# Gate and up projections of three feed-forward groups by seven block products in place of eight

## The chip, the cores and the metric

The kernel runs on one NeuronCore of a Trainium2 chip. The time is device microseconds of one launch on that core; a kernel's time is the median of several runs. Engines are named as in the profile: PE (TensorE matmul), PEld (its weight load), DVE (VectorE), ACT (ScalarE), POOL (GpSimd), SP (SyncE, which issues most loads).

## The reference

A trunk of two layers on 256 tokens of width 1024, in float32:

```python
for l in range(DEPTH):
    x = x + 0.5 * swiglu(rms_norm(x, ffn1_norm[l]), ffn1_w_gate[l], ffn1_w_up[l], ffn1_w_down[l])
    ...   # projection, windowed and differential attention, output projection
    x = x + 0.5 * swiglu(rms_norm(x, ffn2_norm[l]), ffn2_w_gate[l], ffn2_w_up[l], ffn2_w_down[l])
return rms_norm(x, final_norm)

def swiglu(h, w_gate, w_up, w_down):
    return (jax.nn.silu(h @ w_gate) * (h @ w_up)) @ w_down
```

The feed-forward width is 2816. There are four feed-forwards in all, and the change touches only them.

## The kernel before

Every float32 matrix is used as a sum of two float32r parts, a high part (the rounded value) and a low part (what is left). A product of two such matrices takes three matmuls: high by high, low by high, high by low. One matmul has a 128x128 stationary block of activations (128 tokens) and 512 columns of weights as the moving operand; it adds into one PSUM bank of 128x512.

The 2816 columns of a feed-forward are cut into five groups of 512 and a rest of 256. For group n the main loop (line 642) computes gate and up of the 256 tokens (two banks each, `tokens`, line 470: 8 blocks of the inner dimension, 2 token halves, 3 matmuls, so 48 matmuls for gate and 48 for up), turns the hidden values of the group before (`turn`, line 609: eight PE transposes, then a split into high and low part by ACT and DVE), applies silu on ACT (`gate`) and the product with up on DVE (`up`, line 555), and adds the down product of the group before into four accumulator banks (`down`, line 623: two halves of 24 matmuls). PSUM has eight banks; four of them are the accumulators for the whole feed-forward.

Weights come as a list of steps, `specs`. A plain step is 1 MB: 512 rows by 512 columns. `emit_dma` (line 154) has SP load it into one of six `raw` buffers; `emit_split` (line 167) makes the high part on ACT (two casts of 128x1024, into one of three `whi` buffers) and the low part on DVE (two subtractions of 128x1024, into one of three `wlo` buffers). `weights()` (line 219) hands out the next step's parts, and before that calls `ahead`, which emits the splits up to two steps ahead (`LOOK`), the preparations (`prep`) one step further, and the loads up to eight steps ahead (`AHEAD`) as long as a `raw` buffer is to be had. PE, ACT, DVE and POOL instructions run on each engine in the order in which the program emits them, except in a part of the attention; so where `weights()` is called decides where the casts stand in ACT's and DVE's queues.

The kernel before already holds the code for seven products, but the tuple `SEVEN` (line 31) is empty, so `seven` (line 115), `by_seven` (line 575), `prod` (line 565) and `make_sums` (line 304) are never called. With `SEVEN` empty a group has six weight steps: gate upper and lower rows, up upper and lower rows, and the two halves of down.

Of the kernel before, what the change touches and what calls it, by code (L numbers as in the profile page):

```python
# [27 lines left out]
LOOK, AHEAD = 2, 8  # L28
N_RAW, N_HI, N_LO = 6, 3, 3
N_S4 = 16  # L30
SEVEN = ()


@with_exitstack
def trunk(ctx: ExitStack, tc: tile.TileContext, x, n1, g1, u1, d1, nm, w_in, sink,
# [31 lines left out]
    def nm_(s):  # L67
        uid[0] += 1
        return f"{s}_{uid[0]}"

    def bank():
        return ps.tile([P, 512], F32, tag="ps", bufs=8, name=nm_("ps"))

    def halves(b):
        return b.rearrange("p (a n) -> p a n", a=2)

    def blk(dt=F32R):
        return s4.tile([P, 2, 512], dt, tag="s4", name=nm_("s4"))

    def tmp(tag="tmp", bufs=5, shape=(P, 2, 256), dt=F32):  # L80
        return tp.tile(list(shape), dt, tag=tag, bufs=bufs, name=nm_(tag))
# [137 lines left out]
    def weights(look=LOOK):  # L219
        i = at["use"]  # L220
        at["use"] += 1
        if i > 1:
            ahead(i + look)
        return loaded.pop(i)

    for l in range(DEPTH):
        def ffn_specs(wg, wu, wd):
# [3 lines left out]
            for g in range(1, NGRP):  # L231
                downs = [down(g - 1, h) for h in range(2)]
                if g in SEVEN:
                    specs.extend(seven(wg[l], wu[l], g * 512, downs))
# [38 lines left out]
    class Norm:  # L273
# [30 lines left out]
        def make_sums(self):  # L304

            self.sm = []

            def part(b, t):

                vs = [f(self.xs[2 * b + i]) for i in range(2)]  # L310
                return [[v[:, :, c + t * P:c + (t + 1) * P] for v in vs] for c in (0, S)]

            def make(x, y, op, rest):
                v = tmp().rearrange("p a (c s) -> p (a c) s", c=2)
                for i in range(2):
                    vi = v[:, 2 * i:2 * i + 2]
                    dve.tensor_tensor(vi, x[i], y[i], op=op)
                    for z, o in rest:
                        dve.tensor_tensor(vi, vi, z[i], op=o)
                sm = blk().rearrange("p a (c s) -> p (a c) s", c=2)  # L320
                act.copy(sm[:, :, 0:P], v)
                dve.tensor_tensor(sm[:, :, P:S], v, f(sm[:, :, 0:P]), op=ALU.subtract)
                self.sm.append(sm)
                return [v[:, 0:2], v[:, 2:4]]

            add, sub = ALU.add, ALU.subtract
            (t0h, t0l), (t1h, t1l), (b0h, b0l), (b1h, b1l) = [part(b, t) for b in range(2) for t in range(2)]
            s1 = make(b1h, t1h, sub, [(b1l, add), (t1l, sub)])
            s2 = make(s1, t0h, add, [(t0l, add)])
            make(t1h, t0h, sub, [(t1l, add), (t0l, sub)])  # L330
            make(b0h, s2, sub, [(b0l, add)])

        def quarter(self, t, b):

# [48 lines left out]
    norm = Norm(0)  # L383
# [86 lines left out]
    def tokens(accs, xs, w, k0, ks=range(4), first=0, last=KC - 1, order=None):  # L470

        hi, lo = w
        for k, t in (order or [(k, t) for k in ks for t in range(2)]):
            kk = k0 + k
            xv = xs[kk // 2][:, kk % 2]
            xh, xl = xv[:, t * P:(t + 1) * P], xv[:, S + t * P:S + (t + 1) * P]
            pe.matmul(accs[t], lhsT=xh, rhs=hi[:, k], start=kk == first, stop=False)
            pe.matmul(accs[t], lhsT=xl, rhs=hi[:, k], start=False, stop=False)
            pe.matmul(accs[t], lhsT=xh, rhs=lo[:, k], start=False, stop=kk == (last if isinstance(last, int) else last[t]))
# [63 lines left out]
    def ffn(norm, aside=None, before=None, final=False):  # L543
        def silu(out_, acc, t):
            act.activation(out_, acc, AF.Silu, scale=norm.r[:, t:t + 1])
            return out_

        def gate(gs):
            g = []
            for t in range(2):  # L550
                n = gs[t].shape[1]
                g.append(silu(tmp().rearrange("p a n -> p (a n)")[:, :n], gs[t], t))
            return g

        def up(h, acc, g, t):
            n = acc.shape[1]
            dve.scalar_tensor_tensor(h[:, t, :n], in0=acc, scalar=norm.hr[:, t:t + 1], in1=g, op0=ALU.mult, op1=ALU.mult)

        def hidden(g, us):
            h = blk(F32)  # L560
            for t in range(2):
                up(h, us[t], g[t], t)
            return h

        def prod(xo):
            hi, lo = weights()
            acc = bank()
            for k in range(4):
                xh, xl = xo(k)
                pe.matmul(acc, lhsT=xh, rhs=hi[:, k], start=k == 0, stop=False)  # L570
                pe.matmul(acc, lhsT=xl, rhs=hi[:, k], start=False, stop=False)
                pe.matmul(acc, lhsT=xh, rhs=lo[:, k], start=False, stop=k == 3)
            return acc

        def by_seven(h, g):

            flat = lambda: tmp().rearrange("p a n -> p (a n)")

            def put(o, x, y, op):
                dve.tensor_tensor(o, x, y, op=op)  # L580
                return o

            p1 = prod(norm.quarter(0, 0))
            m1 = flat()
            act.copy(m1, p1)
            p7 = prod(norm.summed(2))
            hT = turn(h, 2)
            p6 = prod(norm.summed(1))
            u2 = put(flat(), p6, m1, ALU.subtract)
            u3 = put(flat(), p7, u2, ALU.add)  # L590
            down(hT, g - 1, 0, weights())
            h = blk(F32)
            p2 = prod(norm.quarter(0, 1))
            g0 = put(m1, p2, m1, ALU.add)
            silu(g0, g0, 0)
            p4 = prod(norm.quarter(1, 1))
            g1 = put(flat(), p4, u3, ALU.subtract)
            silu(g1, g1, 1)
            p5 = prod(norm.summed(0))
            put(u3, u3, p5, ALU.subtract)  # L600
            put(u2, u2, p5, ALU.subtract)
            up(h, u3, g1, 1)
            p3 = prod(norm.summed(3))
            put(u2, u2, p3, ALU.add)
            up(h, u2, g0, 0)
            down(hT, g - 1, 1, weights())
            return h

        def turn(hs, n):
            out_ = []  # L610
            for i in range(n):
                sl = halves(bank())
                for c in range(2):
                    for t in range(2):
                        pe.transpose(sl[:, c, t * P:(t + 1) * P], hs[:, t, (2 * i + c) * P:(2 * i + c + 1) * P], ident)
                hb = blk()
                split(hb, sl)
                out_.append(hb)
            return out_

        accs = [[bank(), bank()] for _ in range(2)]

        def down(hT, g, h, w):
            tokens(accs[h], [None] * (2 * g) + hT, w, 4 * g, last=(FC - 1, G4 - 1) if final and h else FC - 1)


        gs, us = [bank(), bank()], [bank(), bank()]
        if before is None:
            before = norm.late
        before(0)  # L630
        ws = (weights(), weights(LOOK - 1))
        for k in (0, 2):
            if k:
                before(1)
            for sl, w in zip((gs, us), ws):
                tokens(sl, norm.xs, w, 0, (k, k + 1))
        before(2)
        tokens(gs, norm.xs, weights(), 4)
        g = gate(gs)
        tokens(us, norm.xs, weights(), 4)  # L640
        h = hidden(g, us)
        for n in range(1, NGRP):
            if n + 1 == min(SEVEN, default=0):
                norm.make_sums()
            if n == 3 and aside is not None:
                aside()
            if n in SEVEN:
                h = by_seven(h, n)
                continue
            gs = [bank(), bank()]  # L650
            tokens(gs, norm.xs, weights(), 0)
            hT = turn(h, 2)
            tokens(gs, norm.xs, weights(), 4)
            g = gate(gs)
            us = [bank(), bank()]
            for k0 in (0, 4):
                tokens(us, norm.xs, weights(), k0)
            h = hidden(g, us)
            for hh in range(2):
                down(hT, n - 1, hh, weights())  # L660

        gu = [bank(), bank()]
        tokens(gu, norm.xs, weights(), 0)
        hT = turn(h, 2)
        tokens(gu, norm.xs, weights(), 4)
        h = hidden(gate([b[:, 0:256] for b in gu]), [b[:, 256:512] for b in gu])
        return accs, hT, lambda: turn(h, 1)
# [278 lines left out]
    for l in range(DEPTH):  # L946
# [7 lines left out]
        if not final:  # L954
            norm = Norm((l + 1) * 8)
# [71 lines left out]
```

## Time and profile before

| | us |
|---|---|
| median of 3 runs | 964.41 (964.31 to 964.84) |
| profiled execution | 964.2 |
| its span on the core | 962.4 |
| PE busy in the span | 951.3 |
| DVE busy | 557.4 |
| ACT busy | 478.2 |
| POOL busy | 20.1 |

Times in the views are microseconds from the start of the span. In a timeline row stand the start, the time of the merged instructions, the engine, the line (here always that of a helper, L50), the operation, output and input tiles, shapes, the count, and the idle time before with what ended it. In a row of grouped instructions stand the count, then busy time and mean nanoseconds of one, then idle time before. In a row of DMA issues stand the count, the size of one and the median time from issue to landing. In a row by stretches stand, for each engine, the busy time and the number of instructions, then the granted clock of PE, the share of time that the DMA engines were busy, and GB/s.

### The profile page before, as it was taken

The numbers are of one execution on the slowest core, as the hardware profiler recorded it, in microseconds if no ns is written. First come the engines' busy times: TensorE is split into PE (matmuls) and PEld (weight loads), VectorE is DVE, ScalarE is ACT, GpSimd is POOL, SyncE is SP. The second block draws the span as 40 slices with busy tenths as digits, with TensorE's granted clock in tenths as the row PEclk, the third lists the DMA queues.
The fourth block names the chain that finished last, engine by engine and source line by source line (L and its number), as shares of the span: only waits on it lengthen the run. The fifth ranks groups of instructions, "written<-read, shape, count | busy, mean of one in ns | idle before, by whom it ended". The sixth has DMA issues, their size and how long they took to land.

```text
span 962.4 us, 12393 instructions
## 1 busy us (share of the span) xinstructions
PE 951.3 (99%) x4940; PEld 807.9 (84%) x4940; DVE 557.4 (58%) x854; ACT 478.2 (50%) x781; POOL 20.1 (2%) x49
## 2 busy tenths in 40 slices
PE   8999999999999999999999999999999999999997
PEld 6888888899888888888888888888999888888886
DVE  5555545579756555545665445556796665445453
ACT  7544444467735543443554434435676464434443
POOL 0300000000000000000000000000000000000001
PEclk9999999999999999999999999999999999999998
DMA  9965555655425565555556555556551446565501
GB/s 338 329 218 175 177 187 204 176 176 132 132 91 173 188 205 179 192 188 185 174 180 210 179 185 198 183 176 179 172 174 47 161 150 214 175 227 189 175 1 44
DMA packets 98218, 169.39 MB, mean 176 GB/s; under 512 B 3182, under 2 KB 30896, under 8 KB 98160
## 3 DMA queue, kind: packets, MB, share of 16 engines
q1 hardware_dynamic: 96816, 167.27, 52.2%
q0 software_dynamic: 256, 0.29, 0.4%
q10 hardware_dynamic: 1088, 1.05, 0.3%
q8 instruction: 38, 0.62, 0.3%
q14 instruction: 20, 0.16, 0.0%
HBM read 167.54 MB, written 1.05 MB: 175 GB/s over the span
## 4 chain that ended last, share of the span: by engine, by line
PE 98%; DMA 0%; issue 0%; DVE 0%; ACT 0%; POOLq 0%; POOL 0%; ACTq 0%; DVEq 0%
PE ps L50 98%; DMA xk<-in_x_dram 0%; DVE s L50 0%; ACT tmp L50 0%; DVE xk L50 0%; POOLq L1022 0%; POOL rf L50 0%; ACTq L50 0%; DVE rf L50 0%; DVEq L50 0%
## 5 line engine op out<-in xcount | busy, mean ns | idle before, releaser
L50 PE MATMUL ps<-whi,s 128*128 128x512 f32 (+1 forms) x2316 | 717.5, 391 | 0.0
L50 DVE TENSOR_TENSOR wlo<-raw,whi 128x1024 fp32r<-128x1024 f32 (+2 forms) x392 | 378.6, 1014 | 237.7 <-ACT whi L50 234.7
L50 PEld LDWEIGHTS ps<-whi,s 128*128 128x128 f32 x2316 | 431.2, 188 | 87.2 <-ACT whi L50 0.3
L50 ACT CAST whi<-raw 128x1024 fp32r<-128x1024 f32 (+2 forms) x392 | 323.9, 884 | 264.0 <-PE ps L50 245.0
L50 PE MATMUL ps<-wlo,s 128*128 128x512 f32 x1158 | 450.2, 389 | 0.0
L50 PEld LDWEIGHTS ps<-wlo,s 128*128 128x128 f32 x1158 | 217.7, 188 | 45.4 <-DVE wlo L50 0.4
L50 PE MATMUL ps<-s,whi 128*128 128x256 f32 x448 | 82.7, 286 | 0.0
L50 ACT CAST s<-ps 128x512 fp32r<-128x512 f32 x48 | 26.0, 589 | 97.4 <-PE ps L50 97.4
L50 DVE TENSOR_TENSOR s<-ps,s 128x512 fp32r<-128x512 f32 x48 | 31.1, 687 | 72.9 <-ACT s L50 72.9
L50 PEld LDWEIGHTS ps<-s,whi 128*128 128x128 f32 x448 | 70.1, 192 | 1.1
L50 PE MATMUL ps<-s,wlo 128*128 128x256 f32 x224 | 63.3, 283 | 0.0
L50 ACT ACTIVATE tmp<-ps,r 128x512 f32<-128x512 f32 (+1 forms) x48 | 30.8, 654 | 46.9 <-PE ps L50 46.8
L50 DVE SCALAR_TENSOR_TENSOR s<-ps,hr,tmp 128x512 f32<-128x512 f32 (+1 forms) x48 | 32.4, 705 | 31.8 <-PE ps L50 25.4
L50 PEld LDWEIGHTS ps<-s,wlo 128*128 128x128 f32 x224 | 42.9, 192 | 0.0
L50 PE MATMUL ps<-ident,s 128*128 128x128 f32 x304 | 39.6, 273 | 0.0
L50 PEld LDWEIGHTS ps<-ident,s 128*128 128x128 f32 x304 | 35.1, 141 | 4.7
L50 ACT ACTIVATE s<-s,negm 128x256 f32<-128x256 f32 x64 | 31.9, 501 | 7.4 <-DVE negm L50 7.4
L50 ACT ACTIVATE s<-ps,gcol 128x256 fp32r<-128x256 f32 x48 | 19.3, 473 | 19.1 <-PE ps L50 19.0
L50 DVE SCALAR_TENSOR_TENSOR s<-ps,gcol,s 128x256 fp32r<-128x256 f32 x48 | 20.3, 477 | 12.5 <-ACT s L50 12.4
L50 POOL TENSOR_TENSOR r<-ms,mhalf 128x2 f32<-128x2 f32 x6 | 4.2, 707 | 629.9 <-DVE ms L50 629.9
L50 ACT ACTIVATE junk<-xk 128x512 f32<-128x512 f32 x24 | 15.3, 637 | 0.4
L50 PE MATMUL ps<-vA,s 128*128 128x64 f32 x128 | 14.7, 273 | 0.0
(93 smaller groups left out, 269.8 us busy)
## 6 DMA issues: line engine op xcount, KB each, us to landing
raw<-in_ffn_w_down_dram SPq DMA_DIRECT2D x44, 1024.0 KB, 4.9
raw<-in_ffn_w_gate_dram SPq DMA_DIRECT2D x39, 1024.0 KB, 5.0
raw<-in_ffn_w_up_dram SPq DMA_DIRECT2D x39, 1024.0 KB, 5.0
raw<-in_w_in_dram SPq DMA_DIRECT2D x14, 1024.0 KB, 5.1
raw<-in_ffn_w_gate_dram SPq DMA_DIRECT2D x8, 512.0 KB, 3.6
raw<-in_ffn_w_up_dram SPq DMA_DIRECT2D x8, 512.0 KB, 4.6
raw<-in_w_in_dram SPq DMA_DIRECT2D x8, 512.0 KB, 4.5
raw<-in_w_out_dram SPq DMA_DIRECT2D x4, 1024.0 KB, 4.8
```

Of the source, the lines that this page charges most:

```text
L50: ins = issue(*a, **k)
```

## The change

In groups 2, 3 and 4 of every feed-forward, gate and up are computed together as a product of a 2x2 block matrix of activations (token half by half of the inner dimension) with a 2x2 block matrix of weights, by Winograd's form of Strassen's method: seven block products of 12 matmuls each (`prod`), where the plain way takes eight.

With a the gate's upper rows, b and c the up's upper and lower rows, and d the gate's lower rows, the nine weight steps of such a group are, in order: a (product p1), b+c (p7), a+b+c (p6), the first half of down, d (p2), a+b+c+d (p4), a+b (p5), c (p3), the second half of down. b+c is made by a load of b and an accumulating DMA of c onto it, issued by POOL (`gather`, line 125; it is emitted right behind b's load). a+b+c and a+b+c+d are made by DVE (`plus`, line 130: two additions of 128x1024 each). a+b is made by another accumulating DMA from POOL, of b onto a, emitted after a's cast and after the addition that reads a. So b and c are read from HBM twice.

On the activations' side, four sums of token and inner-dimension blocks are made once for each feed-forward (`make_sums`): on DVE 20 operations of 256 columns, four low parts of 512, on ACT four casts of 512. The change emits them in four portions between the steps of group 1.

The products are combined by one ACT copy and seven DVE operations of 128x512 (`put`), and silu and `up` follow as before.

Against the code that is there, three things are changed: `SEVEN` is set to (2, 3, 4); `make_sums` becomes a generator whose portions are emitted one by one in group 1; and in `by_seven` the call of `weights()` is taken out of `prod`, so that from p2 on the next step's casts are emitted ahead of silu and `up`, while the copy of p1's bank and the sums u2 and u3 stay ahead of the casts that follow them.

```diff
-SEVEN = ()
+SEVEN = (2, 3, 4)
...
             s1 = make(b1h, t1h, sub, [(b1l, add), (t1l, sub)])
+            yield
             s2 = make(s1, t0h, add, [(t0l, add)])
+            yield
             make(t1h, t0h, sub, [(t1l, add), (t0l, sub)])
+            yield
             make(b0h, s2, sub, [(b0l, add)])
+            yield
...
-        def prod(xo):
-            hi, lo = weights()
+        def prod(xo, w):
+            hi, lo = w
             acc = bank()
...
-            p1 = prod(norm.quarter(0, 0))
+            p1 = prod(norm.quarter(0, 0), weights())
             m1 = flat()
             act.copy(m1, p1)
-            p7 = prod(norm.summed(2))
+            p7 = prod(norm.summed(2), weights())
             hT = turn(h, 2)
-            p6 = prod(norm.summed(1))
+            p6 = prod(norm.summed(1), weights())
             u2 = put(flat(), p6, m1, ALU.subtract)
             u3 = put(flat(), p7, u2, ALU.add)
             down(hT, g - 1, 0, weights())
             h = blk(F32)
-            p2 = prod(norm.quarter(0, 1))
+            p2 = prod(norm.quarter(0, 1), weights())
             g0 = put(m1, p2, m1, ALU.add)
+            w = weights()
             silu(g0, g0, 0)
-            p4 = prod(norm.quarter(1, 1))
+            p4 = prod(norm.quarter(1, 1), w)
             g1 = put(flat(), p4, u3, ALU.subtract)
+            w = weights()
             silu(g1, g1, 1)
-            p5 = prod(norm.summed(0))
+            p5 = prod(norm.summed(0), w)
             put(u3, u3, p5, ALU.subtract)
             put(u2, u2, p5, ALU.subtract)
+            w = weights()
             up(h, u3, g1, 1)
-            p3 = prod(norm.summed(3))
+            p3 = prod(norm.summed(3), w)
             put(u2, u2, p3, ALU.add)
+            w = weights()
             up(h, u2, g0, 0)
-            down(hT, g - 1, 1, weights())
+            down(hT, g - 1, 1, w)
             return h
...
         for n in range(1, NGRP):
-            if n + 1 == min(SEVEN, default=0):
-                norm.make_sums()
+            sums = norm.make_sums() if n + 1 == min(SEVEN, default=0) else iter(())
...
             g = gate(gs)
+            next(sums, None)
             us = [bank(), bank()]
             for k0 in (0, 4):
                 tokens(us, norm.xs, weights(), k0)
+                next(sums, None)
             h = hidden(g, us)
             for hh in range(2):
                 down(hT, n - 1, hh, weights())
+                if hh == 0:
+                    next(sums, None)
```

## The prediction

> **What bounds the kernel now.** I read the page's busy shares and chain first, then the busy time by stretches for groups 2 to 4 of the first feed-forward, then the timelines of PE, DVE and ACT in the same place, then the groups by shape, the DMA queues and the waits of SP's queue.
>
> ```profile
> span 962.4 us, 12393 instructions
> PE 951.3 (99%) x4940; PEld 807.9 (84%) x4940; DVE 557.4 (58%) x854; ACT 478.2 (50%) x781; POOL 20.1 (2%) x49
> PE 98%; DMA 0%; issue 0%; DVE 0%; ACT 0%; POOLq 0%; POOL 0%; ACTq 0%; DVEq 0%
> ```
>
> ```profile
> core 0: us, PE busy (x) PEld busy (x) DVE busy (x) ACT busy (x) POOL busy (x), PEclk, DMA share, GB/s
> 103.30:136.80 33.50, 33.50 (x153) 27.86 (x152) 17.78 (x17) 15.53 (x17) 0.00 (x0) 1.00 0.59 192
> 136.80:170.30 33.50, 33.50 (x153) 27.84 (x152) 16.88 (x16) 14.25 (x16) 0.00 (x0) 1.00 0.56 190
> ```
>
> ```profile
> 103.33 1.03 PE L50 MATMUL ps<-ident,s 128*128 128x128 f32 x8
> 104.12 0.71 PE L50 MATMUL ps<-whi,s 128*128 128x512 f32 x2
> 104.67 0.39 PE L50 MATMUL ps<-wlo,s 128*128 128x512 f32 x1
> 104.90 0.62 PE L50 MATMUL ps<-whi,s 128*128 128x512 f32 x2
> 105.35 0.39 PE L50 MATMUL ps<-wlo,s 128*128 128x512 f32 x1
> 105.58 0.62 PE L50 MATMUL ps<-whi,s 128*128 128x512 f32 x2
> ```
>
> The whole chain is PE, so each matmul that goes is worth its pitch as long as PE is fed. Three matmuls start every 105.58 - 104.90 = 0.68 us, 0.227 each. A group of 144 matmuls takes 32.64 us, and its eight transposes some 0.86 (103.33 to 104.12, and a longer first matmul behind them): 33.5, the stretch that repeats at the full clock. DVE works 16.88 us of that, so it idles half the time. The reader is to see that half: it is what the change spends.
>
> ```profile
> 104.58 1.29 DVE L50 TENSOR_TENSOR s<-ps,s 128x512 fp32r<-128x512 f32 x2 [0.38 <-ACT s L50]
> 106.02 2.36 DVE L50 TENSOR_TENSOR wlo<-raw,whi 128x1024 fp32r<-128x1024 f32 x2
> 111.52 2.36 DVE L50 TENSOR_TENSOR wlo<-raw,whi 128x1024 fp32r<-128x1024 f32 x2 [3.14 <-ACT whi L50]
> 120.06 1.43 DVE L50 SCALAR_TENSOR_TENSOR s<-ps,hr,tmp 128x512 f32<-128x512 f32 x2 [1.54 <-PE ps L50]
> L50 DVE TENSOR_TENSOR wlo<-raw,whi 128x1024 fp32r<-128x1024 f32 x256 | 302.1, 1222 | 227.6 <-ACT whi L50 224.6
> L50 DVE TENSOR_TENSOR s<-ps,s 128x512 fp32r<-128x512 f32 x48 | 31.1, 687 | 72.9 <-ACT s L50 72.9
> L50 DVE TENSOR_TENSOR wlo<-raw,whi 128x256 fp32r<-128x256 f32 x32 | 11.1, 419 | 0.0
> 103.96 1.07 ACT L50 CAST s<-ps 128x512 fp32r<-128x512 f32 x2 [1.21 <-PE ps L50]
> 109.18 1.37 ACT L50 ACTIVATE tmp<-ps,r 128x512 f32<-128x512 f32 x2 [0.94 <-PE ps L50]
> 110.44 1.99 ACT L50 CAST whi<-raw 128x1024 fp32r<-128x1024 f32 x2
> ```
>
> **PE's part of the change.** Gate and up of a group take 84 matmuls in place of 96; the down products and transposes stay. A group goes from 33.5 to 132 x 0.227 + 0.86 = 30.8 us. Three groups in four feed-forwards: 12 x 2.72 = 32.6 us is the most there is to gain.
>
> **ACT's part.** Nine weight steps in place of six, at 1.99 us a pair of casts, give 17.9; the copy of p1 about 0.6, the split of the hidden 1.07, two silus 1.37: 21 us of 30.8. It hides. Were it in the way, the place would be the silus, which the change puts behind the next cast, so that a cast no longer waits for a gate that DVE has still to make. The moved calls also issue loads earlier in program order, but on SP's queue these stand behind their buffers in any case (the row of 736 us below).
>
> **DVE's part** is the dear one. Per group: nine pairs of low-part subtractions, and two pairs of inner sums (line 134) of the same size with both inputs in SBUF, for which the subtraction is the nearest row: 11 x 2.36 = 26.0. Seven operations on product banks at 0.69: 4.8. The hidden split 1.29, the two last products 1.43. Sum 33.5. Independent neighbours overlap by some 0.08 (two of 1.222 take 2.36), so a busy DVE could do it in 32. I take 33.1, since half the neighbours depend on each other or on another engine. Either way DVE now has more work than PE's 30.8 and paces the group.
>
> That the excess isn't paid in full comes from where DVE starts. The three `whi` buffers let a cast begin only when the step three before it is through. So in group 2, when p2 starts, DVE has nothing to do until the cast of p5's weights is half done (1.0, say 1.1 us later). From there to the last down product of group 4, DVE has two whole groups (66.2) and three pairs and two bank operations (8.2): 75.5 us after p2's start. PE alone would be there after two and a half groups less one down product: 16.32 + 14.47 + 16.32 + 14.47 + 10.88 = 72.5 (first half of a group: three products of 2.72, transposes, a down of 5.44; second: four products and a down). PE so loses 3.0 us a feed-forward, of 3 x 2.72 = 8.16 gained. Net 5.1, four times 20.5 us. With DVE at 32.0 a group the loss is 0.9 (29 us gained), at 33.5 it is 3.8 (17 us). Where the lag is paid: the hidden split stands in DVE's queue behind the plus, `up`, and two casts' subtractions, and the first down product waits for it.
>
> The inner operand sums before group 2 are 20 operations of 256 columns at 0.42 and four of 512 at 0.69: 11 us of DVE in group 1, which has 33.5 - 16.9 = 16.6 free, in four portions of at most 3.3 between casts two steps ahead. I cost them at nothing; without that cover they would be 44 us in all. PSUM has four banks beside the accumulators: p6 needs p1's, which the copy on ACT frees some 2 us ahead, and later products find one free; I cost that at nothing, and a late copy would stop PE for what it is late. The tail after group 4 has downs of 5.44 us a cast, where DVE catches up.
>
> **DMA's part.** Six loads a group become eight: two of them are accumulations of 1 MB issued by POOL, of which the trace of before has none.
>
> ```profile
> q1 hardware_dynamic: 96816, 167.27, 52.2%
> raw<-in_ffn_w_up_dram SPq DMA_DIRECT2D x39, 1024.0 KB, 5.0
> grow<-in_ffn_norm_dram SPq DMA_DIRECT2D x1, 8.0 KB, 2.5
> grow<-in_ffn_norm_dram POOLq DMA_DIRECT2D x1, 8.0 KB, 5.0
> s<-in_lam_k_dram POOLq DMA_DIRECT2D x2, 64.0 KB, 7.8
> SPq L159 <- DVE wlo L50: 736.2, 139, 20.7
> ```
>
> A load lands in 5.0 us; 52.2% of 962.4 us over 167.27 MB is 3.15 us of all engines per load of 1.049 MB. SP's loads stand waiting for a buffer (736 us in sum), so they start the moment a buffer comes free. The next group's `b` (up, upper rows) gets the buffer that the plus into `d` frees, about 0.6 us before p2 starts; it lands 4.4 us after p2's start, and the accumulation of `c` onto it follows. Its cast must begin 15.2 us after p2's start if the loaded DVE is to find it (in its order: p5's, p3's, down's and the next `a`'s subtractions, five bank operations and an `up` come first, 3.1 + 13.2 = 16.3, less 1.1 for the cast). So the accumulation may take 10.8 us. What comes later moves the subtraction, the plus, `up`, the transposes and the next down by as much; this occurs twice a feed-forward (the first `b` is loaded in group 1, long ahead), eight times in all. Behind the accumulation on POOL's queue stands only the next one, `b` onto `a`, whose sum is cast 13 us after it can start, so the wait on POOL itself costs nothing.
>
> Bounds for the accumulation: below, a plain load's 5.0. From POOL a small transfer landed 2.5 us later than from SP (5.0 against 2.5): 7.5. In its time SP issues the loads that refill two further buffers, so it shares the engines; one load's worth more is 10.6. Above, 7.8 and twice a load's work under an equal share, 4 x 3.15: 20.4. I take 10.6, by the load's row, which has the same size and shape: just hidden. The ends stay for the range: each microsecond over 10.8 costs 8.
>
> The Trainium skill speaks against this (Collectives: The Full Stack, "The bandwidth ceiling: the fold count and why AG ≠ RS ≠ AR"): an add made by the DMA engines reads two sources through one read ring, so it moves at half the rate of a copy. No run here shows it yet; by that the accumulation is an estimated 6.3 us of engines and not 3.15, and the sum would be 956 or 981 in place of 944, as the turns fall (the first two rivals below).
>
> Sum: 964.2 (profiled; span 962.4 and 1.8 around it) - 20.5 = 943.7. The runs' median, 964.41, is 0.2 above the profiled one: **944 us**.
>
> **Rivals.** *The accumulation comes late.* If it occupies the engines for twice a load's 3.15 us and alternates with the two loads behind it, it needs 2 x 6.3 us besides about 2.8 of latency (a little over SP's 2.5 for 8 KB): 15.4, that is 4.6 late, eight times 37 us: 981. It decides from 10.8 + 20.5/8 = 13.4 us from b's landing on; beyond that the kernel is slower than before. For it: two more transfers where DMA is already 56 to 59% busy, and loads that cluster right there. Against it: 8 loads' work of 3.15 is 25 us of 31, even 10 is 31.5, and the engines have idle time in the rest of the group.
>
> *Late, but not by enough.* With double reads but two thirds of the engine time (its turns are longer), 2.8 + 9.5 = 12.3, 1.5 late, eight times 12: 956.
>
> *DVE takes more than its rows.* Every bank operation waits for a matmul's end and every subtraction for a cast; if that adds 2 us a group (35.1), PE loses 1.1 + 70.2 + 8.2 - 72.5 = 7.0 of the 8.16, and 960 is left; it turns slower from 35.7 on. For it: 227.6 us of DVE's idle time stands before those subtractions. Against: that is idle for lack of work, and ACT has a third of its time free.
>
> **How the numbers follow.** Forecast, the accumulation hidden (936 to 950): 0.42. Late, not enough (950 to 962): 0.15, with the heavy DVE 0.06 beside it (950 to 970). The late accumulation (964 to 990): 0.33. Worse than that, 0.04. About 0.2% (2 us) is what a measurement here can tell from no change. Faster by more: 0.42, most of 0.15 and half of 0.06, 0.57 in the sum, which I lower to 0.53, since the schedule was followed by hand and what it misses adds time; same 0.05; slower 0.42. The range 935 to 988 has DVE at 32 to 33.5 with a hidden accumulation at its low end and the late one at its high end. The likeliest case alone is 936 to 950.
>
> **What would show it.** Right: twelve stretches of 31 to 33 us where groups of 33.5 were; DVE near 100% busy from p2 of group 2 to the end of group 4; PE's idle time before weights put down to DVE, some 3 us a feed-forward; accumulations landing 8 to 11 us after issue. Wrong: PE or ACT waiting for `raw` from the POOL queue; second and third groups of 34 us and more; accumulations of 13 us and over; PE idle where DVE is idle too. A DVE below 90% busy there would show that something ahead of it paces the group.

## Result and profile after

The changed kernel takes 979.87 us (979.29 to 981.43, 4 runs), the kernel before beside it 964.62: a ratio of 1.016, 95% interval 1.0143 to 1.0178. It is slower; the forecast was 944, and the first rival, the late accumulation, had 981.

The page of the changed kernel: the span, the busy shares, and the chain of work that ended last, by engine and by line; then the queues' share of the sixteen DMA engines and the accumulations' median time to land.

```profile
span 978.7 us, 12691 instructions
PE 933.0 (95%) x4796; PEld 781.7 (80%) x4796; DVE 778.6 (80%) x1154; ACT 562.3 (57%) x881; POOL 51.0 (5%) x73
PE 53%; DVE 22%; DMA 16%; ACT 5%; issue 4%; POOLq 0%; ACTq 0%; POOL 0%; DVEq 0%
PE ps L50 53%; DMA raw<-in_ffn_w_up_dram 15%; DVE wlo L50 12%; DVE raw L50 3%; ACT whi L50 3%; DVE tmp L50 3%; DVE s L50 3%; ACT s L50 1%; DMA xk<-in_x_dram 0%; ACT tmp L50 0%; DVE distA L50 0%; ACTq L50 0%; DVE xk L50 0%; DVE distB L50 0%; POOLq L1034 0%
q1 hardware_dynamic: 96816, 167.27, 50.1%
q0 software_dynamic: 12928, 25.46, 14.8%
raw<-in_ffn_w_up_dram POOLq DMA_DIRECT2D x24, 1024.0 KB, 8.8
```

There are 144 matmuls fewer, worth 32.6 us, and yet the span is 16.3 us longer: 49 us that PE's work does not explain, some 12 in each feed-forward. PE's idle time rose by 34.6 us of that (from 962.4 - 951.3 to 978.7 - 933.0); the rest lies within its busy rows. A chain that was 98% PE now has 15% in the loads of up's weights, which is where the accumulations are counted.

Busy time by stretches, each from one turning of the hidden values to the next, in the second feed-forward: groups 2, 3 and 4, first before, then changed.

```profile
357.30:390.83 33.53, 33.53 (x153) 27.86 (x152) 16.88 (x16) 14.24 (x16) 0.00 (x0) 1.00 0.56 187
390.83:424.38 33.55, 33.55 (x154) 27.86 (x153) 16.88 (x16) 14.25 (x16) 0.00 (x0) 1.00 0.57 187
424.38:457.91 33.53, 33.53 (x153) 27.85 (x152) 16.88 (x16) 14.25 (x16) 0.00 (x0) 1.00 0.57 189
```

```profile
364.29:399.16 34.87, 31.84 (x142) 25.24 (x140) 31.08 (x34) 20.22 (x24) 2.21 (x3) 1.00 0.85 242
399.16:435.97 36.81, 32.02 (x141) 25.32 (x141) 31.86 (x34) 20.57 (x24) 2.56 (x3) 1.00 0.82 228
435.97:468.22 32.25, 31.28 (x141) 25.62 (x142) 31.71 (x33) 20.76 (x24) 1.10 (x1) 1.00 0.90 282
```

The two stretches that have a group by seven behind them are longer than before; the last one, which has none, is shorter (32.25). DVE works 31 to 32 us in each, so it is not full in the long ones. What it waits for stands in the chain in order of time (start, time, what), between groups 3 and 4 of the first feed-forward:

```profile
117.06 2.28 DVE raw L50 x2
119.34 0.02 issue
119.36 4.91 DMA raw<-in_ffn_w_up_dram
...
124.83 13.71 DMA raw<-in_ffn_w_up_dram
...
138.64 1.06 ACT whi L50
139.71 0.02 issue
139.73 2.36 DVE wlo L50 x2
```

This is the cycle of the rival, piece by piece: the plus into d frees the buffer, SP loads b in 4.9 us, POOL adds c to it in 13.7, the cast follows, then the subtraction. The same cycle comes eight times: its accumulations take 13.1 to 14.5 us, where the other sixteen take 8.1 to 11.1. On DVE's timeline the same moment is a hole of 3.86 us, with nothing between:

```profile
135.19 0.68 DVE L50 TENSOR_TENSOR tmp<-tmp,ps 128x512 f32<-128x512 f32 x1
139.73 2.36 DVE L50 TENSOR_TENSOR wlo<-raw,whi 128x1024 fp32r<-128x1024 f32 x2 [3.86 <-ACT whi L50]
```

The eight holes of this kind are 3.6 to 4.9 us long and sum to 33.2. The row names ACT as releaser; ACT itself had waited for the accumulation, as the chain shows. A row that names the last engine is followed back one step further.

SP's queue in the same place (start, time of the instruction): b's load, and behind it the loads that share the engines with the accumulation issued at 124.83.

```profile
119.36 0.37 SPq L159 DMA_DIRECT2D raw<-in_ffn_w_up_dram  x1
122.95 0.37 SPq L159 DMA_DIRECT2D raw<-in_ffn_w_down_dram  x1
125.22 0.37 SPq L159 DMA_DIRECT2D raw<-in_ffn_w_gate_dram  x1
128.09 0.37 SPq L159 DMA_DIRECT2D raw<-in_ffn_w_up_dram  x1
131.17 0.37 SPq L159 DMA_DIRECT2D raw<-in_ffn_w_down_dram  x1
```

The accumulation's own stretch, with the DMA engines' share second from the end:

```profile
124.83:138.54 13.71, 13.71 (x62) 11.34 (x62) 10.91 (x13) 7.36 (x8) 1.27 (x1) 1.00 1.07 303
```

The engines are busy the whole time, though over the run their share is 65%: the accumulation shares full engines with the loads issued around it.

### The profile page after: what moved, and what is told of

The parts are those of the page before. It is cut to its first block, busy times and chain, and to the rows that moved or that the text cites. A ratio compares the mean times of both kernels' runs of the same rounds, so it can differ in the third digit from the quotient of the medians.

```text
span 978.7 us, 12691 instructions
## 1 busy us (share of the span) xinstructions
PE 933.0 (95%) x4796; PEld 781.7 (80%) x4796; DVE 778.6 (80%) x1154; ACT 562.3 (57%) x881; POOL 51.0 (5%) x73
## 3 DMA queue, kind: packets, MB, share of 16 engines
q1 hardware_dynamic: 96816, 167.27, 50.1%
q0 software_dynamic: 12928, 25.46, 14.8%
## 4 chain that ended last, share of the span: by engine, by line
PE 53%; DVE 22%; DMA 16%; ACT 5%; issue 4%; POOLq 0%; ACTq 0%; POOL 0%; DVEq 0%
PE ps L50 53%; DMA raw<-in_ffn_w_up_dram 15%; DVE wlo L50 12%; DVE raw L50 3%; ACT whi L50 3%; DVE tmp L50 3%; DVE s L50 3%; ACT s L50 1%; DMA xk<-in_x_dram 0%; ACT tmp L50 0%; DVE distA L50 0%; ACTq L50 0%; DVE xk L50 0%; DVE distB L50 0%; POOLq L1034 0%
## 5 line engine op out<-in xcount | busy, mean ns | idle before, releaser
L50 PE MATMUL ps<-whi,s 128*128 128x512 f32 (+1 forms) x2220 | 695.3, 393 | 20.0 <-DVE s L50 8.8
L50 DVE TENSOR_TENSOR wlo<-raw,whi 128x1024 fp32r<-128x1024 f32 (+2 forms) x464 | 461.0, 1043 | 89.4 <-ACT whi L50 87.4
L50 ACT CAST whi<-raw 128x1024 fp32r<-128x1024 f32 (+2 forms) x464 | 396.1, 908 | 203.1 <-DVE raw L50 71.1
L50 PEld LDWEIGHTS ps<-whi,s 128*128 128x128 f32 x2220 | 414.6, 189 | 111.2 <-DVE s L50 13.5
L50 PE MATMUL ps<-wlo,s 128*128 128x512 f32 (+1 forms) x1110 | 434.2, 391 | 4.0 <-DVE wlo L50 4.0
L50 DVE TENSOR_TENSOR raw<-raw,raw 128x1024 f32<-128x1024 f32 x48 | 56.4, 1216 | 0.0
L50 POOL DMA_DIRECT2D raw<-in_ffn_w_up_dram x24 | 31.1, 1295 | 449.5 <-ACT whi L50 298.0
L50 PEld LDWEIGHTS ps<-ident,s 128*128 128x128 f32 x304 | 34.7, 142 | 18.1 <-DVE s L50 14.4
L50 ACT CAST s<-tmp 128x512 fp32r<-128x512 f32 (+1 forms) x22 | 13.2, 601 | 49.1 <-DVE tmp L50 49.1
L50 ACT ACTIVATE s<-s,negm 128x256 f32<-128x256 f32 x64 | 31.8, 499 | 7.4 <-DVE negm L50 7.4
L50 DVE TENSOR_TENSOR tmp<-ps,tmp 128x512 f32<-128x512 f32 x48 | 32.8, 684 | 0.4
L50 ACT ACTIVATE tmp<-tmp,r 128x512 f32<-128x512 f32 x24 | 17.4, 725 | 19.1 <-DVE tmp L50 19.1
```

The source lines that it names most:

```text
L50: ins = issue(*a, **k)
```

## Experiments

### The accumulation taken away, made plain, and made early

```diff
# e1_no_gather_cb
-                Step(4, 512, load(b), key=b, behind=gather(c, b), free=[]),
+                Step(4, 512, load(b), key=b, free=[]),
# e2_pool_plain: the same DMA, from the same queue, without the add
-                pool.dma_start(raws[to], w[k], accum_op=ALU.add)
+                pool.dma_start(raws[to], w[k])      # for c onto b only
# e3_seventh_raw
-LOOK, AHEAD = 2, 8
-N_RAW, N_HI, N_LO = 6, 3, 3
-N_S4 = 16
+LOOK, AHEAD = 2, 9
+N_RAW, N_HI, N_LO = 7, 3, 3
+N_S4 = 14
```

> Leaves out the accumulation of c onto b, so p7, p6 and p4 are made with b alone; everything else as in the changed kernel. Theory A (the late accumulation paces groups 2 and 3): its eight waits go, what stays is DVE's excess of about 3 us a feed-forward and the wait behind the attention constants, about 4 us once: 948 us (942 to 953), with the stretches from one turn to the next at 31 to 33 us. Theory B (DVE's and ACT's queues are too full whatever the loads do): 975 to 980.

Measured: 946.62 us, ratio 0.9811 (0.9795 to 0.9827). Theory A. The same kernel without this one transfer (c is left out of p7, p6 and p4) is faster than before by 18.6 us; its presence costs 33.3, that is 4.2 for each of the eight places where one group by seven follows another, and as much as DVE's eight holes together.

> The accumulation of c onto b becomes a plain load from POOL's queue of the same bytes over b, so the sum is left out. Theory A1 (the accumulation is long because it reads two sources): its time from issue to landing falls from 13.5 us by one load's engine time, 3, to about 10.5, which the schedule hides: 946 to 958 us. Theory A2 (it is long because it is issued from POOL behind SP's loads, whatever it does): it stays over 12 us and the time over 968.

Measured: 947.76 us, ratio 0.9822 (0.9808 to 0.9837): A1. The rows of POOL's transfers of the changed kernel and of this one in the same place, between groups 2 and 3 of the first feed-forward, with the time to land last; under each the share of the queue over the whole run (from which 0.4% of small transfers, the row of before, is taken off).

```profile
raw<-in_ffn_w_up_dram POOLq DMA_DIRECT2D x1, 1024.0 KB, 13.4
```

```profile
raw<-in_ffn_w_up_dram POOLq DMA_DIRECT2D x1, 1024.0 KB, 9.2
q0 software_dynamic: 9856, 25.46, 11.7%
```

The same bytes from the same queue land 4.2 us sooner here without the add; in the eight places the plain transfer takes 8.5 to 9.6 us. In engine time: 14.4% of 978.7 us over 24 accumulations is 5.9 us each, where 50.1% over 167.27 MB gives a plain load 3.07. In the run with twelve of the 24 made plain, 11.3% of 946.0 us is 106.9; less 12 x 5.9, that leaves 3.0 for a plain one from POOL. So the add costs 1.9 times a plain load, whichever queue issues that load. The packets say the same: the queue has 12928 in the changed kernel and 9856 here, so each add has 256 packets more than the plain transfer. This fits the rule of the Trainium skill that the prediction set against the change (Collectives: The Full Stack, "The bandwidth ceiling: the fold count and why AG ≠ RS ≠ AR"): two source reads through one read ring. The page states it of the reducing step of a collective, with a ratio of 1.93. The trace agrees on the ratio; that the read ring is the cause no run here shows.

> Seven raw buffers and loads nine steps ahead (N_S4 14 to make room), nothing left out: b's load gets a buffer when the down half's split is done and not when the plus into d is done, about 6 us earlier. Theory A: the accumulation lands 6 us earlier, DVE's 3.9 us hole before the subtraction of b+c closes, and the time is that of the kernel without this accumulation within 3 us, 945 to 955. Theory B: 975 to 980.

Measured: 949.20 us, ratio 0.9835 (0.982 to 0.9849), with nothing left out. Theory A again, from the other side. The eight accumulations land earlier, in the second feed-forward some 5 and 9 us earlier after the turning: they begin 3.0 and 4.5 us sooner, and they are also shorter (9.9 to 13.9 us in the eight places). The same sizes in the kernel before:

> The kernel before with the sizes of the seventh-buffer run alone (N_RAW 7, AHEAD 9, N_S4 14). Its loads were never late, so 964.5 within 1 us; if these sizes help by themselves, the gain of the seventh buffer isn't that of the accumulation.

Measured: 964.66 us, ratio 1.0002 (0.9992 to 1.0012). The seventh buffer by itself does nothing.

The stretches of groups 2 and 3 with seven buffers:

```profile
357.14:388.74 31.60, 31.11 (x142) 25.54 (x140) 31.44 (x34) 20.67 (x25) 2.65 (x3) 1.00 0.95 267
388.74:420.57 31.83, 31.13 (x141) 25.55 (x140) 31.80 (x34) 20.52 (x24) 2.58 (x3) 1.00 0.93 264
```

DVE, the third pair of busy time and count, is now full: 31.80 of 31.83 us.

### The attention constants

The aside is called after the last turning of group 4 (in the stage of the rest columns) and no longer at the start of group 3.

> The attention constants of the first feed-forward move from the start of group 3 to the last stage, nothing left out. Theory C (ACT's exp, which waits for DVE's reduction of the constants, holds up the copy of p1's bank and so p6): PE's one wait of 4.2 us goes, 976 us. Rival: the late accumulation behind it takes up what is won, under 1 us of change.

Measured: 980.87 us, ratio 1.017 (1.015 to 1.0189), beside 979.87. Group 3 of the first feed-forward, changed kernel and this one:

```profile
105.03:145.08 40.05, 34.04 (x141) 27.25 (x141) 35.20 (x45) 23.61 (x27) 2.62 (x3) 0.91 0.75 210
104.85:141.35 36.50, 33.33 (x140) 26.10 (x141) 31.86 (x34) 20.57 (x24) 2.54 (x3) 0.96 0.83 231
```

The stretch lost 3.5 us as expected, and the run as a whole won nothing. So theory C holds for the stretch and not for the time. Of the 3.5 us, 1.4 come back in the last stage of the same feed-forward, where the constants now lie (from its turning to the next, 11.85 us after 10.43). Some 2 more come back in the second and, above all, the fourth feed-forward, whose code is unchanged; why wasn't found. With the accumulation early the question is put again:

> Seven raw buffers and the late attention constants together, nothing left out. If the constants' wait was covered before by the accumulation that came after it, it is free to show now: 949.2 - 4 = 945 us. If the constants' work costs the same wherever it lies, 949.

Measured: 947.96 us, ratio 0.9831 (0.9816 to 0.9845), against 0.9835 without the move: no difference that the intervals hold. The intervals leave the constants some 2 us at most.

### The order of the kernel before

```diff
-SEVEN = ()
+SEVEN = (2, 3, 4)      # in the kernel before, nothing else
```

> The kernel before with SEVEN = (2, 3, 4) and nothing else of the change: prod calls weights() itself, silu and up ahead of the next casts, the operand sums in one piece. Theory A: the accumulation sets the pace in any order, so the time is that of the changed kernel or some us more, 980 to 990. Rival (the order is what costs): clearly under 975.

Measured: 1004.59 us, ratio 1.0422 (1.0402 to 1.0442), 24.7 us above the changed kernel and beyond the range named. Its stretches of groups 1 to 4 in the second feed-forward, of which the first has the operand sums in one piece:

```profile
339.12:378.51 39.39, 35.49 (x153) 28.74 (x152) 29.57 (x38) 20.20 (x24) 2.61 (x2) 0.96 0.53 144
378.51:410.59 32.08, 31.41 (x142) 25.46 (x141) 28.45 (x31) 16.69 (x19) 1.28 (x1) 1.00 0.85 250
410.59:446.55 35.96, 32.30 (x141) 25.32 (x140) 32.23 (x34) 20.49 (x24) 2.57 (x2) 1.00 0.83 234
446.55:482.48 35.93, 32.29 (x142) 25.33 (x140) 32.22 (x34) 21.92 (x25) 1.28 (x1) 1.00 0.79 236
```

Group 1 makes the whole difference. It takes 39.39 us here and 40.03, 38.74 and 40.92 in the other feed-forwards, where the changed kernel takes 33.5; in sum 24.9. So the sums in portions are what that part of the change was worth.

The three groups by seven sum to 103.97 us, in the changed kernel to 34.87 + 36.81 + 32.25 = 103.93. But it is not the same wait, and the equal sums are a coincidence. DVE's rows in group 3, with the subtraction of b+c at 442.48:

```profile
430.00 2.36 DVE L50 TENSOR_TENSOR wlo<-raw,whi 128x1024 fp32r<-128x1024 f32 x2 [1.74 <-ACT whi L50]
434.68 2.36 DVE L50 TENSOR_TENSOR wlo<-raw,whi 128x1024 fp32r<-128x1024 f32 x2 [1.73 <-ACT whi L50]
442.48 2.36 DVE L50 TENSOR_TENSOR wlo<-raw,whi 128x1024 fp32r<-128x1024 f32 x2
```

The subtraction of b+c does not wait here, and in the other seven places it waits 0.40 us once. DVE stands twice in each of the twelve groups, 1.73 us each, for a cast that is behind a silu in ACT's queue. So the rival is out, and theory A is not borne out either: in the order of the kernel before, the casts behind the silus are late, and the accumulation hides behind that. The changed order takes this wait away, as the prediction's part on ACT had it, and in the changed kernel the accumulation takes its place.

### What paces the groups once the accumulation is hidden

> SEVEN = (2, 4), nothing else: group 3 is computed the plain way, so that no group by seven follows another and b of group 4 is loaded long ahead. Theory A (the late accumulation comes from two such groups in a row): no wait for it, eight groups of 33.5 become 31.0 to 31.7 each, 945 us (942 to 949), less than the changed kernel although a third of the products saved is given back. Rival (a group by seven loses by its own length, accumulations and all): 964.6 + 2/3 of 15 = 975.

Measured: 946.32 us, ratio 0.9809 (0.9793 to 0.9825). Theory A: no two groups by seven in a row, no late accumulation, and eight of them win as much as twelve with the seventh buffer.

> Seven raw buffers and late constants, and the plus of a+b+c into d left out (p4 is made with d alone): 2.3 us less of DVE in each of the twelve groups. Theory D (with the accumulation hidden DVE's 31.5 us a group pace it, PE needs 30.8): the stretch from turn to turn falls from 31.8 to 30.8 to 31.0, some 10 us below the run with the same two edits. Rival (PE's own switches between banks and weights make the 31.8): under 2 us of change.

Measured: 944.41 us, ratio 0.9794 (0.9779 to 0.9809), with p4 made from d alone: 3.5 us below the same edits with the plus, where theory D wanted 10. PE's waits in this run (what waited for what, us in total, times, longest) and the stretch of group 3:

```profile
PE ps L50 <- DVE s L50: 8.3, 13, 1.0
384.69:416.98 32.29, 31.30 (x141) 25.62 (x141) 30.82 (x33) 21.66 (x26) 3.67 (x3) 1.00 0.92 260
```

With the plus the same stretch takes 32.20 us; theory D had it fall to 31. DVE has 1.5 us to spare in it, and PE still stops for `s`, the split hidden values, about once a group. DVE's total isn't all of it. The split's place in its queue is the other candidate, which the last run below tries.

> As the run with seven buffers and late constants, but in the groups by seven the two products of gate and up go from DVE to POOL (1.4 us a group less on DVE; ACT multiplies the gate by the scale, 0.7 us each) and are issued ahead of the next casts. Theory D (DVE's work of 31.7 us paces the groups): stretches of 31.0 and 938 to 942 us. Rival (the wait is for the hidden split, which stands behind four subtractions in DVE's queue): about 1 us of PE's wait a group stays, 945. Against both: POOL reading SBUF beside DVE slows DVE's subtractions, and 950 or more.

Measured: 953.19 us, ratio 0.9878 (0.9863 to 0.9893): neither theory, but the third case. DVE's and POOL's rows in group 3 of the second feed-forward:

```profile
410.15 3.16 DVE L50 TENSOR_TENSOR wlo<-raw,whi 128x1024 fp32r<-128x1024 f32 x2
413.82 3.45 DVE L50 TENSOR_TENSOR wlo<-raw,whi 128x1024 fp32r<-128x1024 f32 x2
409.79 1.29 POOL L50 TENSOR_TENSOR s<-tmp,tmp 128x512 f32<-128x512 f32 x1 [9.46 <-DVE tmp L50]
413.98 2.21 POOL L50 TENSOR_TENSOR s<-tmp,tmp 128x512 f32<-128x512 f32 x1 [2.89 <-DVE tmp L50]
```

A pair of subtractions that takes 2.35 us alone takes 3.16 and 3.45 beside POOL. DVE gives up two operations of 0.74 and loses 0.8 + 1.1. PE now also waits 5.7 us, in eight places, for ACT's copy of p1's bank, which it did not before. The cast ahead of that copy (at 418.49) had waited 6.01 us for DVE's plus, so this is DVE's lateness again and not ACT's two additional multiplications.

> As the run with up on POOL, and the turning of the hidden values is put ahead of p7, so that their split stands ahead of the down weights' subtractions in DVE's queue. Rival theory (the split's place in the queue): PE's wait before the first down product, about 1 us in each of twelve groups, goes, and the time is 934 to 937. Theory D: within 1.5 us of the run before it.

Measured: 947.40 us, ratio 0.9824 (0.9809 to 0.9838), 5.8 below the run before it. The split's place matters, though PE's wait was taken up in part by another one: its wait for ACT's copy of p1's bank grew from 5.7 to 10.0 us, again in eight places. POOL's toll stayed (pairs of 3.16 and 3.45 us). So the last run has the turn first without POOL, where the groups by seven stand apart:

```diff
# e12, with SEVEN = (2, 4)
-            p7 = prod(norm.summed(2), weights())
             hT = turn(h, 2)
+            p7 = prod(norm.summed(2), weights())
```

> SEVEN = (2, 4) and the turning of the hidden values ahead of p7, nothing left out. If the split's place in DVE's queue is what PE waits for in group 2 (0.5 us of wait and 0.3 of restart, four times), 943 us against the 946.3 of the same groups without it. If DVE's work ahead of the first down product is what counts, or the copy of p1's bank takes the split's place as the late one, 946 to 947.

Measured: 942.48 us (942.03 to 943.28, 5 runs), ratio 0.9772 (0.9758 to 0.9786), nothing left out. The second feed-forward from the turning in group 1 to that in group 3, and from there to that of the last stage; each stretch holds one plain group's time and one by seven:

```profile
318.92:383.28 64.36, 64.36 (x293) 53.49 (x292) 58.93 (x73) 36.83 (x43) 2.60 (x2) 1.00 0.73 218
383.28:447.64 64.36, 64.36 (x293) 53.50 (x292) 49.03 (x50) 35.04 (x39) 2.57 (x2) 1.00 0.81 240
```

PE is busy throughout, and 64.36 less a plain 33.54 leaves 30.82 for the group by seven: the 132 matmuls and the transposes and nothing else. Against the same two groups with the split in its old place (946.32) the move wins 3.8 us, the 3 that were expected of it. Eight groups at 2.72 are 21.8 us; against the kernel before beside it, 964.36 - 942.48 = 21.9. This version beats both kernels.

## Why the prediction was wrong

The step that failed is "I take 10.6, by the load's row, which has the same size and shape: just hidden". The accumulation onto b took 13.4 and 13.7 us where it was read above, and 13.1 to 14.5 in the eight places. The row of a plain load was the wrong one to lean on, because an add is 1.9 times a load's engine time; the plain transfer from POOL did take 9.2, between the 7.5 and the 10.6 of the estimate. The first rival had the mechanism, its place and nearly its size: 15.4 us and 981.

The tolerance of 10.8 us, which I counted from b's landing, was a little too wide as well. In the chain above b landed at 124.27 and POOL issued the accumulation 0.56 us later, a gap that I had left out; it landed 13.71 us after that. DVE stood for 3.86, so 10.4 us from b's landing were hidden, and 9.9 to 10.4 in the eight places. By my own numbers 14.3 us from b's landing would have cost 8 x 3.5 = 28; it cost 33.3. DVE reaches the place sooner than I had it: it needs 31.8 us a group and not 33.1. So the rival of a DVE that takes more than its rows did not come either.

Right was PE's part (30.8 us for a group of 132 matmuls, seen whole in the last run), and nearly right what was left with the accumulation out of the way: 20.5 us was expected and 18.6 measured. But that is in part luck. With DVE at 31.8 my sum would have had PE lose 0.4 us a feed-forward (1.1 + 63.6 + 8.2 - 72.5). The second one with seven buffers lost 2.8 (31.60 + 31.83 + 31.80 less three times 30.82). A DVE that I had too slow made up for a wait that I had in the wrong place. I had PE lose nothing in group 2 and the rest later, since DVE's excess had to build up. With seven buffers group 2 already takes 31.60: the split of the hidden values, which the prediction did name as the place where the lag is paid, waits there behind four subtractions whether DVE has a lag or not. The last run, with the split moved ahead, has no such wait.

The inner operand sums at nothing: right for the changed kernel (its group 1 takes 33.5), since they come in portions; in one piece they cost 24.9. That the copy of p1's bank "would stop PE for what it is late" came true in group 3 of the first feed-forward, where an exp for the constants stood ahead of it, and in the two runs with POOL.

Not settled: where 2 of the 3.5 us of the moved constants went, and how far the turn put first would carry three groups in a row without POOL; that wasn't run.

## What to carry to other kernels

A transfer that adds as it lands cost two loads here, and it is to be costed at the place where it lies on a cycle of buffer, load, add and cast: the engines' share was 65% over the run and full in that place. When such a cycle is late by a few microseconds each time round, another buffer or a plain stage between two such stages takes it off, and both did here. And when an engine is nearly full, its total decides less than what stands in its queue ahead of the one result that PE needs next.

## What the runs showed of the hardware

POOL and DVE slow each other when both read two operands from SBUF: DVE's pair of subtractions went from 2.35 to 3.16 and 3.45 us. POOL's product takes 1.29 us where it starts 0.36 us ahead of the pair, and 2.21 where it starts 0.16 us behind it. The Trainium skill has this (SBUF — State Buffer, "Who interferes with whom"): a DVE instruction with two inputs in SBUF contends with a GpSimd instruction that reads SBUF. The rows above agree and give the size.

A long wait of PE costs more than itself. In the changed kernel's first feed-forward the weights' matmul at 110.31 had waited 4.18 us; the wait and the stretches behind it, with the granted clock third from the end:

```profile
110.31 1.22 PE L50 MATMUL ps<-whi,s 128*128 128x512 f32 x2 [4.18 <-ACT tmp L50]
106.10:110.31 4.21, 0.03 (x2) 0.00 (x1) 3.43 (x11) 2.62 (x5) 0.09 (x1) 0.81 0.86 140
110.31:115.59 5.28, 5.28 (x13) 4.13 (x13) 5.27 (x6) 4.70 (x6) 0.00 (x0) 0.50 0.62 119
115.59:121.03 5.44, 5.44 (x25) 4.51 (x24) 5.41 (x7) 2.11 (x2) 0.00 (x0) 1.00 0.53 182
```

After the wait the clock stays at 0.50 for 5.3 us of full work. The twelve matmuls of p6 take 5.28 us there, the 24 of the down product after them 5.44, so some 2.6 us are lost on top of the 4.2. The Trainium skill describes such a gate (TensorE: Matmul & The Clock Gate, "Part 1: The HAM clock gate (the "warmup" mystery)"): an idle window of about 3.4 us halves the clock, and a busy one restores it. The trace agrees here, and so does the stretch of 39.39 at 0.96, which held a wait of 3.38 us.

But the clock also falls without so long a wait. In the run with the constants late, the stretch of 36.50 us quoted above, at 0.96, ends with waits of 1.47 and 0.53 us (at 136.02 and 137.28), and soon after them the clock is at 0.50:

```profile
139.00:140.00 1.00, 1.00 (x4) 0.81 (x3) 1.00 (x2) 0.39 (x1) 0.00 (x0) 0.50 0.03 8
```

In the changed kernel waits of 1.77 and 0.53 us (at 430.64 and 431.90) left it at 1.00. What decides between the two no run here shows.
